# The front of a two-layer hybrid trunk step: order of loads, norm, conditioning blocks and first projections

## The chip, the cores and the metric

One core of a Trainium2 chip runs the kernel; the other cores are idle. The metric is the device time of one execution in microseconds, the median of several. The engines are named as the profile names them: PE is TensorE, DVE is VectorE, ACT is ScalarE, POOL is GpSimd, and SP is the engine that issues most of the loads and stores.

## What is computed

One inference step of a trunk of two layers, a Mamba-2 layer and a pooling layer, for 1024 prompt tokens and 8 sequences of 8 sample tokens, 1088 columns in all; the model is 1024 wide. Each layer begins in the same way, and only the beginning of the first layer is touched:

```python
sc  = silu(c)                                  # 9 conditioning rows: 8 samples, 1 prompt
mod = sc @ ada_w[i] + ada_b[i]
shift, scale, gate = split(mod, 3)
hn  = x * rsqrt(mean(x*x) + EPS) * norm_g[i] * (1 + scale) + shift
zxbcdt = hn @ w_in                             # z, x, B, C and the 32 step sizes dt
```

Behind it come the convolution, the scan over chunks, the gated norm, the output product and the pooling layer, all as before.

## The kernel before, in words

Activations lie with channels on partitions: `xs[k]`, k = 0..7, is a 128x1088 tile of x. Every product in full precision is split: an activation into `hh` (rounded to fp32r) and `hl` (the rest), a weight into a high and a low tile, and `mm1` (L187 to L192) issues three matmuls for one k and one chunk of columns. `CH` cuts the 1088 columns into 368, 368 and 352.

`setup` (L202) loads c, the eight x tiles, the vector constants `vec` and the other constants `kc` on SP, and issues 62 matmuls of ones (`warm`, L241) that keep TensorE active until data is there. `front` (L1394) then does the following.

- Sum of squares: ACT squares each x tile (L1403, L1407), DVE adds them into `rst` (L1408), the last in three chunks. For each chunk a matmul with ones adds over the partitions (L302, in `ms_log`), ACT takes the logarithm (L305) and the exponential (L318), which leaves 1/rms in `rst`.
- adaLN blocks: `ada_first(kt)` makes shift and scale of x tile kt. `ada_block` (L248) loads two halves of 512 KB (L257), makes eight small matmuls on 32-column strips of the array (L261, tile `am`; the profile shows two records for each), ACT copies the result to `mp` (L266), two tiny matmuls transpose it with constants of `kc` (L270), and DVE writes `shf` (L280) and `scl` (L281).
- `modulate(0, k, ...)` (L320): DVE multiplies x by scale and 1/rms (L325), ACT adds the shift and rounds (`hh`, L331), DVE makes the rest (`hl`, L332), ACT adds the shift to x itself (L333). The 64 sample columns have their own five small operations (L338 to L342).
- The loop over k: for each k the adaLN block of k + 2, `modulate` of k, 18 matmuls for the first two weight tiles of z (`pst`, named mm and p in the trace), and four strip matmuls of the step sizes (L1443, `pdt`), which read the unrounded x that L333 left. The first two weight tiles come whole (L121) and are split whole (L141, L145).
- Then come two more z tiles (`mm` with wh and wl), during which `act_sums_front` (L1471 to L1475) forms sums of x for the fast products that follow. POOL makes the sums of weights for those products (L1035 to L1042).

The order in which an engine executes is fixed before the launch: a scheduler takes, for each engine, the instruction that it expects to be ready, earlier ones in program order first. `tc.issue_after(ins)` adds that what is traced in its block stands behind `ins` on the same engine; it adds no wait for its end.

## Time and profile before

| | us |
|---|---|
| median of 3 runs (1590.49 to 1592.91) | 1590.76 |
| the profiled execution, its device time | 1591.15 |
| its span in the trace | 1589.0 |
| PE busy | 1568.2 |
| DVE busy | 1301.7 |
| ACT busy | 790.1 |
| POOL busy | 525.5 |

The span is what lies between the first and the last instruction of the trace; the 2.15 us beside it belong to launch and end. Times in the rows are counted from the start of the span. Matmuls overlap, so a busy time of PE is no proof of full use; the distance from one matmul's start to the next says more. In the rows of the timeline the columns are start, duration, engine, line, operation, tiles, shape, count, and in brackets the idle time before with what ended it. Rows of one kind that follow each other are merged, and then the duration is that of the whole run.

### The profile page before, as it was taken

How to read it: one execution, taken by the hardware profiler on the slowest of the kernel's cores; microseconds unless marked ns; L12 is line 12 of the kernel's file. 1: busy time of each engine (PE TensorE's matmuls, PEld its weight loads, DVE VectorE, ACT ScalarE, POOL GpSimd, SP SyncE). 2: the span in 40 equal slices, each digit the busy share in tenths (PEclk: the TensorE clock that was granted, in tenths of full speed). 3: DMA queues.
4: the chain of work that ended last, by engine and by line, in shares of the span. 5: the costliest groups of instructions: out<-in, count | busy, mean ns of one | idle time of the engine just before them, and what ended most of it. 6: DMA issues, size and time to landing. Idle time of an engine off the chain costs nothing.

```text
span 1589.0 us, 30720 instructions
## 1 busy us (share of the span) xinstructions
PE 1568.2 (99%) x11946; PEld 1505.1 (95%) x11946; DVE 1301.7 (82%) x2152; ACT 790.1 (50%) x1512; POOL 525.5 (33%) x558
## 2 busy tenths in 40 slices
PE   9999999999999999999999999999999999999997
PEld 7899999999999999989999999999999999999997
DVE  6874889887899989889888858988889777667886
ACT  6663344466766666665456348433333233233373
POOL 0133456522331413141211232366666530000241
PEclk9999999999999999999999999999999999999999
DMA  9422232365555565679999432232333379565783
GB/s 356 167 101 101 80 112 84 111 194 173 161 179 165 162 209 167 212 259 297 311 332 320 164 127 69 85 121 100 117 115 115 104 250 365 140 180 178 163 172 117
DMA packets 122304, 275.57 MB, mean 173 GB/s; under 512 B 18192, under 2 KB 59312, under 8 KB 122160
## 3 DMA queue, kind: packets, MB, share of 16 engines
q1 hardware_dynamic: 118128, 260.90, 48.4%
q0 software_dynamic: 4032, 12.72, 4.7%
q8 instruction: 94, 1.54, 0.4%
q14 instruction: 50, 0.41, 0.1%
HBM read 201.12 MB, written 70.23 MB: 171 GB/s over the span
## 4 chain that ended last, share of the span: by engine, by line
PE 85%; DVE 6%; issue 3%; DMA 3%; ACT 2%; POOL 1%; SPq 0%; DVEq 0%; ACTq 0%; POOLq 0%
PE st L1070 11%; PE st L1072 11%; PE st L1071 11%; PE mm L190 10%; PE mm L191 10%; PE mm L192 10%; PE op L1289 2%; PE op L1291 2%; PE op L1290 2%; PE y L641 2%; PE S L619 2%; PE y L645 1%; PE am L261 1%; PE tr L580 1%; PE tr L577 1%
## 5 line engine op out<-in xcount | busy, mean ns | idle before, releaser
L1072 PE MATMUL st<-hh,w 128*128 128x272 f32 x832 | 240.2, 289 | 0.0
L1070 PE MATMUL st<-hh,w 128*128 128x272 f32 x832 | 240.0, 288 | 0.0
L1071 PE MATMUL st<-hl,w 128*128 128x272 f32 x832 | 240.0, 288 | 0.0
L1070 PE MATMUL st<-t,w 128*128 128x272 f32 x624 | 179.6, 288 | 0.0
L1072 PE MATMUL st<-t,w 128*128 128x272 f32 x624 | 179.5, 288 | 0.0
L1071 PE MATMUL st<-t,w 128*128 128x272 f32 x624 | 179.2, 287 | 0.0
L190 PE MATMUL mm<-hh,wh 128*128 128x368 f32 (+1 forms) x528 | 178.9, 339 | 0.0
L191 PE MATMUL mm<-hl,wh 128*128 128x368 f32 (+1 forms) x528 | 174.0, 330 | 0.0
L192 PE MATMUL mm<-hh,wl 128*128 128x368 f32 (+1 forms) x528 | 173.2, 328 | 0.0
L1070 PEld LDWEIGHTS st<-hh,w 128*128 128x128 f32 x832 | 156.7, 188 | 0.0
L1071 PEld LDWEIGHTS st<-hl,w 128*128 128x128 f32 x832 | 156.7, 188 | 0.0
L1072 PEld LDWEIGHTS st<-hh,w 128*128 128x128 f32 x832 | 156.5, 188 | 0.0
L182 ACT ACTIVATE w<-wr 128x512 fp32r<-128x512 f32 x104 | 64.9, 629 | 165.5 <-PE st L1072 134.2
L627 POOL TENSOR_TENSOR hd<-h,cd 128x256 f32<-128x256 f32 x56 | 46.1, 824 | 285.9 <-DVE h L628 135.6
L1289 PE MATMUL op<-b,w 128*128 128x272 f32 x448 | 129.4, 289 | 0.0
L1290 PE MATMUL op<-b,w 128*128 128x272 f32 x448 | 128.8, 287 | 0.2 <-DVE b L1218 0.2
L1291 PE MATMUL op<-b,w 128*128 128x272 f32 x448 | 128.9, 288 | 0.0
L190 PE MATMUL mm<-gh,wh 128*128 128x368 f32 (+1 forms) x372 | 125.3, 338 | 0.0
L192 PE MATMUL mm<-gh,wl 128*128 128x368 f32 (+1 forms) x372 | 122.4, 329 | 0.0
L191 PE MATMUL mm<-gl,wh 128*128 128x368 f32 (+1 forms) x372 | 122.2, 328 | 0.1
L1070 PEld LDWEIGHTS st<-t,w 128*128 128x128 f32 x624 | 117.6, 189 | 0.1
L1072 PEld LDWEIGHTS st<-t,w 128*128 128x128 f32 x624 | 117.3, 188 | 0.0
(310 smaller groups left out, 4596.9 us busy)
## 6 DMA issues: line engine op xcount, KB each, us to landing
wr<-win SPq DMA_DIRECT2D x48, 512.0 KB, 3.8
wr<-pin SPq DMA_DIRECT2D x32, 512.0 KB, 3.8
acb<-acd SPq DMA_DIRECT2D x60, 256.0 KB, 4.4
wr<-pout SPq DMA_DIRECT2D x28, 512.0 KB, 5.2
x<-x1d SPq DMA_DIRECT2D x24, 544.0 KB, 6.7
x1d<-x SPq DMA_DIRECT2D x22, 544.0 KB, 6.2
wr<-pout POOLq DMA_DIRECT2D x20, 512.0 KB, 6.0
x<-xT SPq DMA_DIRECT2D x16, 544.0 KB, 6.7
```

Source lines behind the costliest of these rows:

```text
L182: self.last_hi = self.nc.scalar.activation(hi, src, AF.Copy)
L190: nc.tensor.matmul(ps[:, :n], hi[:, k, :], ah[:, a:a + n], start=first, stop=False)
L191: nc.tensor.matmul(ps[:, :n], hi[:, k, :], al[:, a:a + n], start=False, stop=False)
L192: nc.tensor.matmul(ps[:, :n], lo[:, k, :], ah[:, a:a + n], start=False, stop=last)
L619: nc.tensor.matmul(S[:, 256 * i:256 * i + 256], Bt, xde.rearrange("p r q -> p (r q)"), start=True, stop=True)
L627: nc.gpsimd.tensor_tensor(out=hd, in0=h[-1], in1=cd.unsqueeze(2).to_broadcast([P, 4, 64]), op=ALU.mult)
L1070: nc.tensor.matmul(ps[c][:, :QUART], hi[:, k], xh[:, t], start=(k == 0), stop=False)
L1071: nc.tensor.matmul(ps[c][:, :QUART], hi[:, k], xl[:, t], start=False, stop=False)
L1072: nc.tensor.matmul(ps[c][:, :QUART], lo[:, k], xh[:, t], start=False, stop=(k == 3))
L1289: nc.tensor.matmul(ps[:, :QUART], hi[:, k], xh, start=k == 0, stop=False)
L1290: nc.tensor.matmul(ps[:, :QUART], hi[:, k], xl, start=False, stop=False)
L1291: nc.tensor.matmul(ps[:, :QUART], lo[:, k], xh, start=False, stop=k == 7)
```

## The change

Loads: x tile 1 and c are issued by ACT, the rest by SP. Of `kc` only the 10 columns for the tiny transposing matmuls come first, then adaLN block 0, `vec`, and parts 0 and 1 (of 8) of the first two weight tiles; then adaLN block 1, the weights' other parts, block 2, `wdt` and the rest of `kc`. Blocks 3 to 7 are loaded from within the loop.

Norm: DVE adds squares 1 to 6 only; the eighth tile's squares are added on TensorE, as a second matmul into the same PSUM tile, chunk by chunk. The adaLN block 0 stands on TensorE behind the first two chunks, the third chunk's two matmuls stand around its transposing matmuls.

Weights: the first two tiles are split in parts 0-1, 2-3 and 4-7, each where it is near its use; the low half of 4-7 on POOL. The sample columns' product with 1/rms is made for all eight tiles on POOL.

Loop: k = 0 and k = 1 are modulated by chunks, and k = 0 runs chunk by chunk over both weight tiles. Block 1 stands behind the third group of matmuls of k = 0, block 2 behind the first group of k = 1. For k = 1 to 5 the step-size matmuls of k - 1 and then the adaLN block of k + 2 stand behind the matmuls of k; the step sizes of 5, 6 and 7 stand behind the matmuls of 7. ACT adds the shift to x one step later. `warm` has 52 matmuls instead of 62, and 4 instead of 8 later. The constants `cwh`, `adab1` and `an` are made later.

```diff
-        nc.sync.dma_start(ct, io["cT"])
         self.xs = []
         for k in range(8):
             t = self.slots.get("x")
-            nc.sync.dma_start(t, io["xT"][k])
+            if k == 1:
+                nc.scalar.dma_start(ct, io["cT"])
+            (nc.scalar if k == 1 else nc.sync).dma_start(t, io["xT"][k])
             self.xs.append(t)
+        self.adaq = []
+        self.kc = cp.tile([P, K_N], F32, tag="kc", name="kc")
+        self.kc_load(K_SEL9, K_SEL64)
+        self.ada_load(0)
         self.vec = cp.tile([P, V_N], F32, tag="vec", name="vec")
         nc.sync.dma_start(self.vec, io["vec"])
-        self.kc = cp.tile([P, K_N], F32, tag="kc", name="kc")
-        nc.sync.dma_start(self.kc, io["kc"])
...
+        self.wfirst = [self.wp.tile([P, 8, P], F32, tag="wr", bufs=3, name=self.name("wr")) for _ in range(2)]
+        self.first_load(0, 2)
...
-        self.warm(62)
+        self.warm(52)
...
+    def ada_load(self, m):
+
+        for hh in range(2):
+            self.adaq.append(self.slots.get("ada"))
+            self.nc.sync.dma_start(self.adaq[-1][:, :1024].rearrange("p (a b) -> p a b", a=4), self.io["adaA"][0, m][:, 4 * hh:4 * hh + 4, :])
+
+    def kc_load(self, a, e):
+
+        self.nc.sync.dma_start(self.kc[:, a:e], self.io["kc"][:, a:e])
+
+    def first_load(self, a, e):
+
+        for i, t in enumerate(self.wfirst):
+            self.nc.sync.dma_start(t[:, a:e], self.items[i][0][:, a:e])
+
+    def first_split(self, raw):
+
+        self.wslots += [self.slots.get("w0", F32R) for _ in range(2)]
+        hi, lo = (t[:, :1024].rearrange("p (k m) -> p k m", k=8) for t in self.wslots[-2:])
+
+        def part(a, e):
+            self.nc.scalar.activation(hi[:, a:e], raw[:, a:e], AF.Copy)
+            return lambda: (self.nc.gpsimd if a == 4 else self.nc.vector).tensor_tensor(out=lo[:, a:e], in0=raw[:, a:e], in1=hi[:, a:e].bitcast(F32), op=ALU.subtract)
+
+        return hi, lo, part
...
-                raws.append(self.slots.get("ada"))
-                nc.sync.dma_start(raws[hh][:, :1024].rearrange("p (a b) -> p a b", a=4), src[:, 4 * hh:4 * hh + 4, :])
+                raws.append(self.adaq.pop(0))
...
-            nc.scalar.activation(t[:, :pn], t[:, :pn], AF.Identity, bias=sh)
         if pn < n:
             s = slice(NP, TOK)
             ts = t[:, pn:n].rearrange("p (b i) -> p b i", i=8)
             eng = nc.gpsimd if l and k % 2 == 0 else nc.vector
-            eng.tensor_tensor(out=t[:, pn:n], in0=x[:, s], in1=rst[:, s], op=ALU.mult)
-            eng.tensor_tensor(out=ts, in0=ts, in1=self.scl[l][:, k, 0:8].unsqueeze(2).to_broadcast([P, 8, 8]), op=ALU.mult)
+            if l:
+                eng.tensor_tensor(out=t[:, pn:n], in0=x[:, s], in1=rst[:, s], op=ALU.mult)
+            with contextlib.nullcontext() if l else self.tc.issue_after(self.mod_x.ins):
+                eng.tensor_tensor(out=ts, in0=ts, in1=self.scl[l][:, k, 0:8].unsqueeze(2).to_broadcast([P, 8, 8]), op=ALU.mult)
             eng.tensor_tensor(out=ts, in0=ts, in1=self.shf[l][:, k, 0:8].unsqueeze(2).to_broadcast([P, 8, 8]), op=ALU.add)
...
         rst = sl.get("rst")
+        after = self.tc.issue_after
+        ms = [self.mm_tile() for _ in CH]
+
+        def add_up(c, sq, start):
+            a, n = CH[c]
+            return nc.tensor.matmul(ms[c][:, :n], self.ones, sq[:, a:a + n], start=start, stop=not start).ins
+
+        def root(c):
+            a, n = CH[c]
+            nc.scalar.activation(rst[:, a:a + n], ms[c][:, :n], AF.Ln, bias=self.eps, scale=1.0 / 1024)
+            return lambda: self.rstd(rst[:, a:a + n])
+
         with self.ln_set():
             nc.scalar.activation(rst, xs[0], AF.Square)
             for k in range(1, 8):
                 sq = self.raw_tile()
                 for a, n in CH if k == 7 else ((0, TOK),):
                     nc.scalar.activation(sq[:, a:a + n], xs[k][:, a:a + n], AF.Square)
-                    nc.vector.tensor_tensor(out=rst[:, a:a + n], in0=rst[:, a:a + n], in1=sq[:, a:a + n], op=ALU.add)
-            for a, n in CH:
-                self.ms_log(rst, rst, a, n, 1.0 / 1024, "mm", 3)
-                self.rstd(rst[:, a:a + n])
-        self.ada_first(0)
+                for a, n in CH if k == 6 else ((0, TOK),) if k < 6 else ():
+                    added = nc.vector.tensor_tensor(out=rst[:, a:a + n], in0=rst[:, a:a + n], in1=sq[:, a:a + n], op=ALU.add)
+            for c in range(2):
+                add_up(c, rst, True)
+                mm = add_up(c, sq, False)
+            self.adab1 = self.cp.tile([P, 48], F32, tag="adab1", name="adab1")
+            with after(added.ins):
+                nc.vector.tensor_scalar(self.adab1, self.vec[:, V_ADAB:V_ADAB + 48], 1.0, None, op0=ALU.add)
+            root(0)()
+            exp = root(1)
+            blk = self.ada_shift_scale(0, 0, False)
+            with after(mm):
+                next(blk)
+            with after(self.mp.ins):
+                exp()
+            with after(self.am):
+                add_up(2, rst, True)
+            for _ in blk:
+                pass
+            with after(self.sel):
+                mm = add_up(2, sq, False)
+            self.wslots = []
+            firsts = [self.first_split(t) for t in self.wfirst]
+            with after(self.mp.ins):
+                lower = [firsts[0][2](0, 2)]
+                exp = root(2)
+                exp()
+                lower.append(firsts[1][2](0, 2))
+        for t in xs:
+            nc.gpsimd.tensor_tensor(out=t[:, NP:TOK], in0=t[:, NP:TOK], in1=rst[:, NP:TOK], op=ALU.mult)
         self.hn = []
-
-        self.wslots = []
-        lower = [self.stream_split(i, True) for i in range(2)]
-        with self.tc.issue_after(self.sel):
-            self.warm(8, "mm", 3)
-        self.ada_first(1)
-        ws = [self.wsplit.pop(i) for i in range(2)]
+        with after(mm):
+            self.warm(4)
+        self.ada_load(1)
+        self.first_load(2, 8)
+        self.ada_load(2)
+        wdts = sl.get("wdt")
+        wdt = wdts[:, :256].rearrange("p (k m) -> p k m", k=8)
+        nc.sync.dma_start(wdt, io["wdt"])
+        self.kc_load(0, K_SEL9)
+        self.kc_load(K_SEL64, K_N)
+        ws = [f[:2] for f in firsts]
         self.wpos = 2
         pst = [[self.mm_tile() for _ in range(3)],
                [self.pp.tile([P, 512], F32, tag=t, bufs=b, name=self.name("p0")) for t, b in (("y", 2), ("y", 2), ("S", 1))]]
         pdt = self.pp.tile([P, 512], F32, tag="tr", bufs=2, name="pdt")
-        for k in range(8):
-            if k < 6:
-                self.ada_first(k + 2)
-            if k == 4:
-                self.stream_split(2)
-            if k == 6:
-                self.stream_split(3)
-            hi, lo = sl.get("hh", F32R), sl.get("hl", F32R)
-            for a, n in CH if k == 0 else ((0, TOK),):
-                last = self.modulate(0, k, xs[k], rst, hi, lo, a, n, xs[k][:, a:a + n])
-                if lower:
-                    lower.pop(0)()
-            self.hn.append((hi, lo))
-            for i in range(2):
-                for c in range(3):
-                    self.mm1(pst[i][c], ws[i], k, (hi, lo), CH[c], k == 0, k == 7)
+
+        def step_sizes(i):
             for j in range(4):
                 n = 320 if j == 3 else 256
-                nc.tensor.matmul(pdt[32 * j:32 * j + 32, :n], wdt[:, k, :], xs[k][:, 256 * j:256 * j + n],
-                                 start=k == 0, stop=k == 7, tile_position=(0, 32 * j))
+                ins = nc.tensor.matmul(pdt[32 * j:32 * j + 32, :n], wdt[:, i, :], xs[i][:, 256 * j:256 * j + n],
+                                       start=i == 0, stop=i == 7, tile_position=(0, 32 * j))
+            return ins
+
+        def unrounded(i):
+            return nc.scalar.activation(xs[i][:, :NP], xs[i][:, :NP], AF.Identity, bias=self.shf[0][:, i, 8:9])
+
+        cwh = self.gp.tile([P, 160], F32, tag="cwh", name="cwh")
+        self.cwh = cwh
+        for k in range(8):
+            if 0 < k < 6:
+                self.ada_load(k + 2)
+            if k in (4, 6):
+                with after(self.mod_hi.ins), after(last.ins):
+                    self.stream_split(k // 2)
+            hi, lo = sl.get("hh", F32R), sl.get("hl", F32R)
+            for a, n in CH if k < 2 else ((0, TOK),):
+                last = self.modulate(0, k, xs[k], rst, hi, lo, a, n, xs[k][:, a:a + n])
+                with after(self.mod_x.ins):
+                    for f in lower:
+                        f()
+                lower = []
+            if k > 1:
+                with after(self.mod_hi.ins):
+                    if k == 2:
+                        for f in firsts:
+                            f[2](4, 8)()
+                    unrounded(k - 1)
+            if k == 2:
+                with after(last.ins):
+                    nc.vector.tensor_scalar(cwh, self.vec[:, V_CW:V_CW + 160], 0.5, None, op0=ALU.mult)
+            self.hn.append((hi, lo))
+            for n, (c, i) in enumerate((c, i) for c in range(3) for i in range(2)) if k == 0 else enumerate((c, i) for i in range(2) for c in range(3)):
+                mm = self.mm1(pst[i][c], ws[i], k, (hi, lo), CH[c], k == 0, k == 7)
+                if k < 2 and n == (2, 0)[k]:
+                    with after(mm.ins):
+                        self.ada_first(k + 1)
+                    if k:
+                        with after(self.mp.ins):
+                            lower = [f[2](2, 4) for f in firsts]
+                            unrounded(0)
+            if 0 < k < 6:
+                with after(mm.ins):
+                    mm = step_sizes(k - 1)
+                with after(mm.ins):
+                    self.ada_first(k + 2)
+        unrounded(7)
+        with after(mm.ins):
+            for k in range(5, 8):
+                step_sizes(k)
```

## Rows read from the trace of the kernel before

**Rows 1.** The page: busy time of TensorE, its share of the span, instructions.

```profile
PE 1568.2 (99%) x11946; PEld 1505.1 (95%) x11946; DVE 1301.7 (82%) x2152; ACT 790.1 (50%) x1512; POOL 525.5 (33%) x558
```

**Rows 2.** Busy time by stretch: length, then five engines, clock, DMA share, GB/s.

```profile
2.00:3.00 1.00, 1.00 (x7) 1.00 (x6) 0.20 (x1) 0.06 (x2) 0.00 (x0) 1.00 0.86 181
...
5.00:6.00 1.00, 1.00 (x8) 1.00 (x7) 0.00 (x0) 0.71 (x1) 0.00 (x0) 1.00 1.02 409
...
68.00:72.00 4.00, 4.00 (x26) 4.00 (x25) 4.00 (x7) 1.77 (x6) 0.00 (x0) 1.00 0.42 166
```

**Rows 3.** Timeline of PE, from the warm matmuls to the first product.

```profile
1.06 16.34 PE L245 MATMUL warm<-ones 128*128 128x128 f32 x124 [1.06 <-DVE ones L217]
...
17.24 1.99 PE L302 MATMUL ms<-rst,ones 128*128 128x368 f32 x6
...
20.32 0.64 PE L261 MATMUL am<-ada,scp 128*32 128x256 f32 x8 [0.52 <-DMA ada<-adaA]
...
21.47 0.61 PE L270 MATMUL am<-kc,mp 128*128 128x9 f32 x4 [0.50 <-ACT mp L266]
...
23.94 0.95 PE L190 MATMUL mm<-hh,w 128*128 128x368 f32 x2
```

**Rows 4.** Timeline of ACT and DVE in the same stretch.

```profile
15.23 1.30 ACT L1407 ACTIVATE raw<-x 128x368 f32<-128x368 f32 x3 [0.28 <-DMA x<-xT]
...
16.55 1.43 DVE L1408 TENSOR_TENSOR rst<-rst,raw 128x368 f32<-128x368 f32 x3
...
21.03 0.38 ACT L266 ACTIVATE mp<-am 128x256 f32<-128x256 f32 x1 [0.18 <-PE am L261]
...
22.65 1.12 DVE L325 SCALAR_TENSOR_TENSOR x<-x,scl,rst 128x368 f32<-128x368 f32 x2
```

**Rows 5.** Timeline of PE in the loop and behind it.

```profile
43.34 0.74 PE L1443 MATMUL pdt<-x,wdt 128*32 128x256 f32 x8
...
48.47 0.75 PE L1443 MATMUL pdt<-x,wdt 128*32 128x256 f32 x8
...
48.93 1.15 PE L261 MATMUL am<-ada,scp 128*32 128x256 f32 x16
...
50.01 0.44 PE L190 MATMUL mm<-hh,w 128*128 128x368 f32 x1
...
62.62 0.74 PE L1443 MATMUL pdt<-x,wdt 128*32 128x256 f32 x8
...
66.46 0.74 PE L1443 MATMUL pdt<-x,wdt 128*32 128x256 f32 x8
...
67.13 0.44 PE L190 MATMUL mm<-hh,wh 128*128 128x368 f32 x1
...
67.41 0.33 PE L191 MATMUL mm<-hl,wh 128*128 128x368 f32 x1
...
71.76 0.33 PE L190 MATMUL mm<-hh,wh 128*128 128x368 f32 x1
```

**Rows 6.** Timeline of ACT and DVE, from adaLN block 6 to the next step.

```profile
50.18 0.39 ACT L266 ACTIVATE mp<-am 128x256 f32<-128x256 f32 x1 [0.84 <-PE am L261]
...
51.59 0.23 DVE L280 TENSOR_SCALAR shf<-am,vec 128x9 f32<-128x9 f32 x1 [0.71 <-PE am L270]
...
52.05 1.28 DVE L325 SCALAR_TENSOR_TENSOR x<-x,scl,rst 128x1024 f32<-128x1024 f32 x1
...
53.37 1.15 ACT L331 ACTIVATE hh<-x,shf 128x1024 fp32r<-128x1024 f32 x1 [0.35 <-DVE x L325]
...
54.78 1.28 DVE L332 SCALAR_TENSOR_TENSOR hl<-x,shf,hh 128x1024 fp32r<-128x1024 f32 x1
```

**Rows 7.** Timeline of POOL and DVE late in the loop, and DVE behind it.

```profile
57.28 1.33 POOL L1036 TENSOR_TENSOR sw<-sw,wr 128x512 f32<-128x512 f32 x1
...
57.37 2.32 DVE L325 SCALAR_TENSOR_TENSOR x<-x,scl,rst 128x1024 f32<-128x1024 f32 x1
...
62.45 1.35 DVE L1471 TENSOR_TENSOR x<-x 128x544 f32<-128x544 f32 x2
```

More of the change, by code (lines that the diff above doesn't have):

```diff
@@ L191, in mm1 @@
         nc.tensor.matmul(ps[:, :n], hi[:, k, :], al[:, a:a + n], start=False, stop=False)
-        nc.tensor.matmul(ps[:, :n], lo[:, k, :], ah[:, a:a + n], start=False, stop=last)
+        return nc.tensor.matmul(ps[:, :n], lo[:, k, :], ah[:, a:a + n], start=False, stop=last)
     def mm3(self, ps, w, acts, ch):
@@ L260, in ada_block @@
             for j in range(4):
-                nc.tensor.matmul(pm[32 * j:32 * j + 32, :256], self.scp[:, j + 4 * hh, :], raws[hh][:, 256 * j:256 * j + 256],
-                                 start=(hh == 0), stop=(hh == 1), tile_position=(0, 32 * j))
+                am = nc.tensor.matmul(pm[32 * j:32 * j + 32, :256], self.scp[:, j + 4 * hh, :], raws[hh][:, 256 * j:256 * j + 256],
+                                      start=(hh == 0), stop=(hh == 1), tile_position=(0, 32 * j))
+        self.am = am.ins
         if src is not None:
@@ L265, in ada_block @@
         mp = self.cp.tile([P, 256], F32, tag="mp", bufs=1, name=self.name("mp"))
-        nc.scalar.activation(mp, pm[:, :256], AF.Copy)
+        self.mp = nc.scalar.activation(mp, pm[:, :256], AF.Copy)
         yield
@@ L472, in dt_phase @@
         an = self.gp.tile([P, 1], F32, tag="an", name="an")
-        nc.scalar.activation(an, self.vec[:, V_ALOG:V_ALOG + 1], AF.Exp)
-        nc.vector.tensor_scalar(an, an, -1.0, None, op0=ALU.mult)
+        with self.tc.issue_after(self.mod_hi.ins), self.tc.issue_after(self.mod_x.ins):
+            nc.scalar.activation(an, self.vec[:, V_ALOG:V_ALOG + 1], AF.Exp)
+            nc.vector.tensor_scalar(an, an, -1.0, None, op0=ALU.mult)
         nc.vector.tensor_scalar(dd, uu, 2.0, None, op0=ALU.add)
```

11 lines of the change are left out of this document (2 added, 9 removed).

## The prediction

> **What bounds the kernel now.** I read the page first: TensorE is busy 1568.2 of 1589.0 us [rows 1], so only time in which TensorE does not do wanted work can be won. Busy time alone would hide that here, because the 62 matmuls of ones count as busy. So the timeline of TensorE comes next: ones until 17.4 us, the norm's three sums at 17.24, the second half of adaLN block 0 at 20.32 after a wait for its load, and the first wanted product only at 23.94 [rows 3]. From there to 67.13, where the next weights begin [rows 5], runs the loop that is changed. Behind it TensorE is full (4.00 of 4.00 us) [rows 2], so what the loop ends earlier, the kernel ends earlier, unless the next stage gives it back.
>
> Inside the loop three distances matter [rows 5]. From 67.41 to 71.76 lie 26 matmuls of 368 columns: 0.167 us each, and by columns 0.160 for 352; one k has 12 and 6 of them, 2.97 us. Step 7, without an adaLN block, takes 66.46 - 62.62 = 3.84, so the step sizes cost 0.87, of which 48.93 - 48.47 = 0.46 is their own and 0.41 is lost in changing tile shape and back. Step 3, with a block, takes 48.47 - 43.34 = 5.13: a block costs 1.29, of which 0.87 for the strips (50.01 - 48.47, against 67.13 - 66.46 without them) and 0.42 for the transposing ones. The loop's own work is thus 8 x 3.84 + 7 x 1.29 = 39.75 us of the 43.19 that it takes. The other 3.44 are waits and block halves standing apart in steps 0 to 2.
>
> **The change: the first product.** The last tile of x is squared from 15.23 on, as it lands, and block 0 is there only at 20.32 [rows 3, 4]. Between the two came block 0 (1.05 MB) and 0.67 MB of constants and step-size weights. At 409 GB/s [rows 2] the block alone needs 2.6 us, so with nearly all constants behind it it lands near 17.8. Two load queues I count at nothing: by 5 us the engines are at a DMA share of 1.02; at 2 to 3 us they show 0.86 with 181 GB/s, which leaves at most about half a microsecond, and the next step would hide it.
>
> That next step is the norm. The three chunk adds of the last tile began at 16.55 and take 1.43, 0.48 each [rows 4]. With tile 6 as the last one on DVE, in chunks, its first chunk is done near 15.5 (16.55, less 0.1 for two constants that move away, less the two chunks of 0.48 behind it). The 52 warm matmuls end between 14.8 (52/62 of 16.34) and 15.7 (if the ten omitted ran at the loop's 0.17). I take 15.7 for the start of the sums. Three chunk sums took 1.99, 0.66 each [rows 3]. Four of them now stand ahead of block 0, the price of adding the last squares here: 15.7 + 2.65 = 18.35, behind the load. From a block's first matmul to its copy on ACT takes 50.18 - 48.93 = 1.25 [rows 5, 6], from the copy to the transposing matmuls 0.44 [rows 3, 4]: 20.04. One more chunk sum of 0.66 stands in between and begins 1.08 after the block, so 20.1. From there to DVE's first modulation took 1.18, and from that to the first product 1.29 [rows 3, 4]: 22.57. The third chunk's logarithm and exponential fall on ACT just there. By the 0.38 for 256 columns [rows 4] one of them in front costs 0.5, none costs 0; I take half. First product at 22.8 (22.6 to 23.1), **1.1 us earlier**.
>
> **The loop's own work.** 8 x 2.97 for the products; six groups of step sizes instead of eight (five beside blocks, one of three at the end), 6 x 0.87 + 2 x 0.46; seven blocks, 7 x 1.29; and blocks 1 and 2 stand alone, two shape changes of 0.41 more. That is 39.75, as before: what the grouping at the end saves, the lone blocks take.
>
> **The waits.** These were 3.44, and here lies the rest of the gain.
>
> Step 1: modulation and rest of step 0 are 1.28 each on DVE when whole [rows 6], about 0.4 more in chunks. Two weight quarters (0.7), the sample columns (0.5) and the next scale and shift (0.46) follow, and POOL's eight products take DVE's turn for 0 to 3 us, say 1.0. From 21.3 that is 26.9, plus 1.2 for the first chunk's modulation and rounding: 28.1. TensorE is through step 0 and block 1 at 22.8 + 2.97 + 1.29 + 0.41 = 27.5. Wait 0.6 (0 to 2). The loads keep up: at 409 GB/s block 1 lands near 21.4 (wanted at 24.6), the weights' other parts near 23.3, block 2 near 25.9 (wanted at 29). For the unrounded x, made a step later on ACT, I count nothing: the step sizes that read it stand behind 18 matmuls; without that cover it would cost its 1.15.
>
> Steps 2 to 6: block k + 2 now stands behind the matmuls of k, one step later than before. The chain after it is in [rows 5, 6]: products go on at 50.01, copy 50.18, shift 51.59, modulation 52.05, rounding 53.37 to 54.52. So the next k can begin 4.5 us after the block. A step with a block and step sizes covers this with 5.13. For what disturbs it I put 0.6 in all (0 to 4): see the rival below.
>
> Step 7: block 7 stands between steps 5 and 6, and step 6 has only 2.97 + 0.42 + 0.1 = 3.5 us of matmuls, since its step sizes are held back until after step 7. The chain of 4.5 is not covered: **a new wait of 1.0**, 0.6 if the transposing matmuls go in at once, 1.4 if the rest (`hl`, another 1.3) is asked for early.
>
> Sum of waits 2.2 instead of 3.44. The loop ends at 22.8 + 39.75 + 2.2 = 64.75 instead of 67.13: 2.4 us. The profiled execution took 1591.15 (span 1589.0 and 2.15 beside it) and would take 1588.75; the median lies 0.39 below it, so the forecast is 1590.76 - 2.4 = **1588.4**. The constants made later on DVE and ACT (0.1 to 0.3 each) come where both have idle time, and are counted at nothing; on the chain at step 7 they would cost those 0.3.
>
> **A rule against the change.** POOL and DVE do get in each other's way: beside POOL's weight sum at 57.28, DVE's modulation took 2.32 instead of 1.28 [rows 6, 7]. Before, this hit step 7's modulation with TensorE far behind, so it cost nothing; now the same chain has 0.6 us of slack, or none. The Trainium skill, "SBUF — State Buffer", section "SBUF: two separate sides", says why: DVE operations with two SBUF inputs and POOL's share one pair of ports under an exclusive lock held for the whole instruction, so that the loser blocks fully rather than slowing down. The row agrees, with 1.04 us lost beside one POOL operation of 1.33. By the rule every product given to POOL could be taken back from DVE in full, and then waits like the slower rival's follow.
>
> **The rivals.**
>
> 1. The waits close. The transposing matmuls go right behind the copy (chain 4.1), POOL falls into DVE's idle time, no exponential stands in front. First product 22.57, waits 0.3 + 0 + 0.6: the loop ends at 63.2, 3.9 us earlier, **1586.9**. For it: in step 3's row shift came 1.4 us after the copy though the copy itself is 0.39 long, so there is room. Against: step 7's missing cover is arithmetic.
>
> 2. Slower. The late blocks and the lock meet: each chain grows by 1.04, to 5.5, and `hl` behind it again, so that steps 2 to 5 wait 1.2 each, step 7 2.0 and step 1 1.7. Waits 8.5, the loop ends at 71.0, **1594.7**. It decides from waits of 4.6 in all (3.44 + 1.1) for a loss, and of 7.8 for a loss one can measure. For it: 57.37 in [rows 7]; POOL's weight sums start as soon as the weight buffers come free, which is earlier now, in steps 4 and 5. Against: POOL has few operations there, and one step's slack of 0.6 takes half of each.
>
> 3. Given back. DVE's sums of x began at 62.45, 4.7 us ahead of the loop's end [rows 5, 7]. Now step 7 begins at 60.0 (64.75 less 2.97 and 1.79), its rest ends near 61.5, and the lead is 3.2. If the next stage needs all of the old lead, 1.5 is lost there: **1589.9**. Against: TensorE has 24 us of ordinary products before the sums are due.
>
> 4. It doesn't do what it says: the scheduler, which knows only expected times, leaves block 0's chain where it was (first product at 23.9, the rest as forecast): **1589.5**.
>
> **How the numbers follow.** Forecast 0.42, rival 1 0.34, rival 2 0.11, rival 3 0.07, rival 4 0.06. About 0.2% (3.2 us) is what a measurement of this kernel can tell from no change, so faster means below 1587.6 and slower above 1593.9. Faster: 0.29 of rival 1 and 0.05 of the forecast's lower end, 0.34. Slower: 0.08, the harder part of rival 2. Same: 0.58. The forecast's own range is 1587.4 to 1590 from its bounds; for 8 in 10 it reaches down through most of rival 1 (1585.5, with the loads earlier as well) and up to rival 2's mild end, 1592.
>
> **What would show it.** First product at 22.8 (right if 22.4 to 23.2); block 0 no longer waiting for its load but for the chunk sums; first product of step 1 about 5.3 us after that; steps 2 to 5 at 5.1 each; TensorE idle for about 1 us ahead of step 7, released by ACT's `hh`; three groups of step sizes at the end, 0.46 apart; next weights at 64.7. I am wrong if TensorE is idle between steps 2 and 6, if step 7 doesn't wait, or if the gain at the loop's end is not there at the end of the span.

## The result and the profile after

The changed kernel takes **1596.69 us** (median; 1594.08 to 1599.08) beside 1591.23 of the kernel before on the same chip: a ratio of 1.0032 [1.0022, 1.0041], so slower by 5.5 us, where 1588.4 was forecast. The profiled execution took 1594.88 with a span of 1592.8.

TensorE's timeline of the changed kernel at the front, to be read against [rows 3] (columns as there):

```profile
1.06 14.53 PE L271 MATMUL warm<-ones 128*128 128x128 f32 x104 [1.06 <-DVE ones L220]
16.45 0.89 PE L1432 MATMUL mm<-rst,ones 128*128 128x368 f32 x2 [0.86 <-DVE rst L1446]
...
19.12 1.07 PE L286 MATMUL am<-ada,scp 128*32 128x256 f32 x16
...
20.82 0.51 PE L296 MATMUL am<-kc,mp 128*128 128x9 f32 x4
...
23.19 0.43 PE L190 MATMUL mm<-hh,w 128*128 128x368 f32 x1 [0.27 <-ACT hh L357]
```

Block 0 no longer waits for its load, and the first product starts at 23.19 instead of 23.94, 0.75 us earlier. The loop behind it loses this and more. The same timeline at those places of the loop where TensorE waits, and the start of the next weights, against [rows 5]:

```profile
24.37 0.43 PE L191 MATMUL mm<-hl,w 128*128 128x368 f32 x1 [0.59 <-DVE hl L358]
...
25.98 1.07 PE L286 MATMUL am<-ada,scp 128*32 128x256 f32 x16
...
30.02 0.43 PE L190 MATMUL mm<-hh,w 128*128 128x368 f32 x1 [0.96 <-ACT hh L357]
...
61.01 0.43 PE L191 MATMUL mm<-hl,w 128*128 128x368 f32 x1 [0.77 <-DVE hl L358]
...
65.84 0.76 PE L190 MATMUL mm<-hh,w 128*128 128x368 f32 x3 [0.81 <-ACT hh L357]
...
71.09 0.43 PE L190 MATMUL mm<-hh,wh 128*128 128x368 f32 x1
```

The next weights start at 71.09 instead of 67.13, 3.96 us later, and the span is 3.8 longer. Behind the loop nothing is lost and nothing given back in these two traces: from the next weights to the span's end lie 1521.9 us before (1589.0 - 67.13) and 1521.7 after. (In the traces of the other kernels below this stretch takes 1519.8 to 1523.2.) So for the profiled execution the answer lies in the eight steps. Their lengths, each from one step's first product to the next one's, and for step 7 to the next weights; "forecast" is the own work of the prediction's sum plus its waits, laid out by step:

| step | 0 | 1 | 2 | 3 | 4 | 5 | 6 | 7 | sum |
|---|---|---|---|---|---|---|---|---|---|
| before | 8.84 | 6.94 | 5.16 | 5.13 | 5.16 | 4.28 | 3.84 | 3.84 | 43.19 |
| forecast, own work | 4.67 | 6.83 | 5.13 | 5.13 | 5.13 | 5.13 | 2.97 | 4.76 | 39.75 |
| forecast with waits | 5.27 | 6.83 | 5.28 | 5.28 | 5.28 | 5.28 | 3.97 | 4.76 | 41.95 |
| after | 6.83 | 6.73 | 6.18 | 5.64 | 5.17 | 5.57 | 6.53 | 5.25 | 47.90 |

Above the own work lie 47.90 - 39.75 = **8.15 us of waits**, where the forecast put 2.2: 2.2 in step 0, 1.05 in step 2, about 0.5 each in steps 3, 5 and 7, and 3.6 in step 6; step 1 gives back 0.1. The kernel before has its 3.44 in steps 0 to 2 and nothing behind them. The changed one still has 3.1 there and 5.0 more in steps 3 to 7. DVE and POOL in step 6:

```profile
57.33 1.22 DVE L145 TENSOR_TENSOR wl<-wr,wh 128x1024 fp32r<-128x1024 f32 x1
58.46 1.30 DVE L366 TENSOR_TENSOR x<-x,scl 128x64 f32<-128x64 f32 x1
59.69 1.27 DVE L358 SCALAR_TENSOR_TENSOR hl<-x,shf,hh 128x1024 fp32r<-128x1024 f32 x1
60.88 1.29 DVE L367 TENSOR_TENSOR x<-x,shf 128x64 f32<-128x64 f32 x1
62.10 0.21 DVE L306 TENSOR_SCALAR shf<-am,vec 128x9 f32<-128x9 f32 x1
...
62.55 0.85 DVE L369 TENSOR_TENSOR hl<-x,hh 128x64 fp32r<-128x64 f32 x1
63.33 1.27 DVE L351 SCALAR_TENSOR_TENSOR x<-x,scl,rst 128x1024 f32<-128x1024 f32 x1
```

```profile
57.62 2.06 POOL L1063 TENSOR_TENSOR sw<-wr 128x512 f32<-128x512 f32 x1 [17.22 <-DMA wr<-win]
59.76 2.33 POOL L1064 TENSOR_TENSOR sw<-sw,wr 128x512 f32<-128x512 f32 x1
62.05 1.26 POOL L1068 TENSOR_TENSOR wr<-wr,wr 128x512 f32<-128x512 f32 x1
```

Operations of 64 columns that take 0.21 to 0.23 elsewhere take 1.30, 1.29 and 0.85 here, and modulation 7 begins only at 63.33; its rounding releases TensorE at 65.84. POOL and DVE take turns: each line of POOL ends about where a stretched line of DVE does, while the two long lines of DVE between them (1.22 and 1.27) keep their length. The Trainium skill, "SBUF — State Buffer", section "SBUF: two separate sides", has this as an exclusive lock held for a whole instruction; the trace agrees, with 0.22 against 1.30 for the same operation.

Step 2 shows the same once more, DVE and then POOL:

```profile
38.55 0.28 DVE L307 TENSOR_SCALAR scl<-am,adab,vec 128x9 f32<-128x9 f32 x1
...
39.17 1.34 DVE L1525 TENSOR_SCALAR cwh<-vec 128x160 f32<-128x160 f32 x1
40.42 1.27 DVE L351 SCALAR_TENSOR_TENSOR x<-x,scl,rst 128x1024 f32<-128x1024 f32 x1
```

```profile
37.44 2.96 POOL L263 TENSOR_TENSOR w<-wr,w 128x512 fp32r<-128x512 f32 x2 [10.54 <-ACT w L262]
```

Scale 3 is there at 38.83, but the constants `cwh`, which take 0.24 with POOL away, hold DVE until modulation 3 begins at 40.42. By these lines the lock can account for step 2's 1.05 as well; no kernel below tests this by itself.

### The profile page after: what moved, and what is told of

It is laid out like the page before. It is cut to its first block, busy times and chain, and to the rows that moved or that the text cites. A ratio compares the mean times of both kernels' runs of the same rounds, so it can differ in the third digit from the quotient of the medians.

```text
span 1592.8 us, 30706 instructions
## 1 busy us (share of the span) xinstructions
PE 1568.8 (98%) x11924; PEld 1504.2 (94%) x11924; DVE 1305.2 (82%) x2149; ACT 790.4 (50%) x1516; POOL 531.2 (33%) x568
## 4 chain that ended last, share of the span: by engine, by line
PE 85%; DVE 6%; issue 3%; ACT 2%; DMA 2%; POOL 1%; SPq 0%; DVEq 0%; ACTq 0%; POOLq 0%
PE st L1098 11%; PE st L1100 11%; PE st L1099 11%; PE mm L190 11%; PE mm L191 10%; PE mm L192 10%; PE op L1317 2%; PE op L1319 2%; PE op L1318 2%; PE y L669 2%; PE S L647 2%; PE y L673 1%; PE tr L608 1%; PE am L286 1%; PE tr L605 1%
```

## The experiments

The theory was that two things together make the loop longer: adaLN blocks that come a step later (late blocks), and POOL's sums of weights beside DVE (the lock). The rivals were that one of them alone does it, that the front does it (loads, ones, clock), or that it is not in the loop. The first four kernels ran with the kernel before on one chip, as did the next four, the next three and the last one.

**The change again.** The changed kernel with no edit.

> The changed kernel as it is, for a second trace and more times. If what the first trace shows is the rule, the steps again start near 23.2, 30.0, 36.8, 42.9, 48.6, 53.7, 59.3, 65.8 us and the next weights near 71.1, 4.0 us later than before. The times went from 1594.1 to 1599.1 with a mean granted clock between 0.998 and 0.995; if the spread belongs to the clock, a trace with the lower one shows a stretch at the lower level, and if it belongs to the waits, the steps start at other times.

Median 1595.93, ratio 1.0028 [1.0017, 1.0040]. The loop took 47.91 with each step as in the first trace, but it began at 25.71 instead of 23.19. The timeline of TensorE, and its clock by stretch (columns as [rows 2]), of this run:

```profile
1.06 13.32 PE L271 MATMUL warm<-ones 128*128 128x128 f32 x104 [1.06 <-DVE ones L220]
17.29 1.16 PE L1432 MATMUL mm<-rst,ones 128*128 128x368 f32 x2 [2.91 <-DVE rst L1446]
18.24 1.43 PE L1432 MATMUL mm<-raw,ones 128*128 128x368 f32 x2
```

```profile
18.00:21.00 3.00, 3.00 (x6) 1.66 (x5) 0.30 (x2) 1.08 (x2) 0.00 (x0) 0.50 1.02 392
```

The ones end at 14.38, TensorE is idle for 2.91 us, and the sums then run at a granted clock of 0.50, the 1.2 GHz level: 1.2 us from one to the next instead of 0.62. First product 2.5 us later: the sums start 0.84 later, and from the first sum to the first product lie 8.42 instead of 6.74. In the first trace of after the ones ended at 15.59, the gap was 0.86 and the clock stayed at 1.00. Three kernels below have the same front (POOL waits, blocks early, and the changed kernel with blocks half a step earlier); with gaps of 2.03 to 2.17 their traces show a clock of 0.83 from 15 to 25 us, as this one does.

**POOL waits.** POOL's first sum of weights waits for DVE's last rest of step 7.

```diff
-            nc.gpsimd.tensor_tensor(out=s[:, f], in0=z[:, f], in1=z[:, l], op=ALU.add)
+            ins = nc.gpsimd.tensor_tensor(out=s[:, f], in0=z[:, f], in1=z[:, l], op=ALU.add)
+            if self.mod7 is not None:
+                self.tc.add_manual_dep(ins.ins, self.mod7.ins.name, ...)
...
+        self.mod7 = last
```

> Only change: POOL's first sum of weights waits until DVE has made the last rest of step 7. Theory (late adaLN blocks meet POOL on the ports that DVE needs): the two small sample operations on DVE in step 6 take 0.22 instead of 1.3 us, modulation 7 begins about 2.5 us earlier, step 7 starts near 63.4 and the next weights near 68.6, 2.5 us before the changed kernel. Rival (late blocks alone, their chain is too long with or without POOL): next weights stay at 70.5 to 71.1. Rival (POOL alone is the cause): next weights at 67 or before.

Median 1594.54, ratio 1.0021 [1.0011, 1.0031]. Step 6 took 4.58 instead of 6.53, and no other step moved by over 0.02. DVE and POOL of this kernel:

```profile
60.13 0.22 DVE L366 TENSOR_TENSOR x<-x,scl 128x64 f32<-128x64 f32 x1
...
61.49 0.22 DVE L367 TENSOR_TENSOR x<-x,shf 128x64 f32<-128x64 f32 x1
...
63.04 1.28 DVE L351 SCALAR_TENSOR_TENSOR x<-x,scl,rst 128x1024 f32<-128x1024 f32 x1
```

```profile
67.04 1.71 POOL L1063 TENSOR_TENSOR sw<-wr 128x512 f32<-128x512 f32 x1 [24.98 <-DVE hl L369]
```

So the lock costs **1.95 us** in step 6. The loop is still 45.94. By its time alone this kernel can't be told from the change, since their intervals overlap.

**Blocks early, in the changed kernel.** Blocks 3 and 4 behind step 1, then block k + 3 behind step k; their loads are issued earlier to match.

```diff
...
-                    self.ada_first(k + 2)
+                    for m in (3, 4) if k == 1 else (k + 3,) if k < 5 else ():
+                        self.ada_first(m)
```

> Only change: adaLN blocks 4 to 7 stand one step earlier (3 and 4 behind step 1, then block k+3 behind the matmuls of k, k = 2 to 4), so that each modulation has a whole step more of cover. Theory: step 1 is longer by a block (1.3 us), then steps 2 to 4 take their own work, 5.1 each, steps 5, 6, 7 take 3.8, 3.1 and 3.0, and the next weights start near 65.5, 5.5 us before the changed kernel and 1.6 before the kernel before. Rival (POOL on the ports is the cause): the waits of 2 us around POOL's sums stay and the next weights start at 68 or later.

Median 1593.38, ratio 1.0009 [0.9998, 1.0019]: 2.6 us better than the change, with intervals that just overlap. Steps 5 to 7 fell from 17.35 to 12.28, of which 1.29 is a block that has left them, but steps 2 and 3 rose from 11.82 to 14.15, where that block now lies. Loop 45.14. POOL's first sum begins only at 63.17 here, behind modulation 7 (61.64), and that modulation keeps its 1.28.

**Blocks late, in the kernel before.** The converse: the kernel before with block k + 2 behind the step sizes of k and nothing else.

```diff
-            if k < 6:
-                self.ada_first(k + 2)
...
+            if k < 6:
+                with self.tc.issue_after(ins.ins):
+                    self.ada_first(k + 2)
```

> The kernel before with one part of the change: each adaLN block of k+2 stands behind the step sizes of k instead of ahead of the matmuls of k. Nothing moves to POOL, loads and norm are the old ones. Theory: steps 0 to 2 hardly change, but modulations 5 to 7 lose their cover, POOL's sums (57 us) now hit the chain of step 7, and the next weights start 2 to 4 us later than 67.1, the kernel is slower by as much. Rival (the new front, its chunks and POOL's new products are the cause): next weights at 67.1 to 67.6, time as before.

Median 1593.47, ratio 1.0015 [1.0005, 1.0025]. The loop took 45.70 instead of 43.19: steps 5 to 7 took 5.55, 4.56 and 5.44 instead of 4.28, 3.84 and 3.84, of which 1.29 is block 7, which now lies there. POOL, DVE, and TensorE's wait in step 7, of this kernel:

```profile
61.75 2.15 POOL L1036 TENSOR_TENSOR sw<-sw,wr 128x512 f32<-128x512 f32 x1
```

```profile
62.67 1.31 DVE L339 TENSOR_TENSOR x<-x,scl 128x64 f32<-128x64 f32 x1
64.02 1.19 DVE L340 TENSOR_TENSOR x<-x,shf 128x64 f32<-128x64 f32 x1
```

```profile
65.55 0.43 PE L190 MATMUL mm<-hh,w 128*128 128x352 f32 x1 [0.96 <-ACT hh L341]
```

The late blocks without the rest of the change thus cost about half of what it loses in the loop (2.5 of 4.7), and they bring the lock with them: POOL's sums, which cost the kernel before nothing, now stretch DVE's operations for the sample columns of step 7, and TensorE waits 0.96 for these. How much of the 2.5 would stay with POOL held back was not tried.

**More ones.** The changed kernel with 62 warm matmuls instead of 52.

```diff
-        self.warm(52)
+        self.warm(62)
```

> The changed kernel with 62 warm matmuls instead of 52, nothing else. Theory (the gap of up to 2.9 us between the 52 matmuls and the first chunk sum is what lowers TensorE's clock in some executions): the gap shrinks to about 1.2 us or closes, the granted clock stays at 1.00 from 15 to 25 us, the first product stands between 23.2 and 24.1, never at 25, and the times spread less, median near 1594.8, with the loop's steps as before (47.9 in all). Rival (the spread comes from elsewhere, as the low stretches near 700 and 1000 us): times spread from 1592.7 to 1599 as with 52.

Median 1595.51, ratio 1.0024 [1.0014, 1.0034]. The clock stayed at 1.00 in the front, but the ones now end at 17.95 and stand in front of the sums; the first product came at 24.42. In step 6 TensorE waited 1.40 us for the sample columns:

```profile
64.71 0.48 PE L190 MATMUL mm<-hh,w 128*128 128x352 f32 x1 [1.40 <-ACT hh L368]
```

Behind this wait the granted clock was 0.66 from 65 to 70 us, and the loop took 48.72. Filling the gap with ones is no repair.

**One load queue.** The changed kernel with c and all of x issued by SP, c first, as before.

```diff
+        nc.sync.dma_start(ct, io["cT"])
...
-            if k == 1:
-                nc.scalar.dma_start(ct, io["cT"])
-            (nc.scalar if k == 1 else nc.sync).dma_start(t, io["xT"][k])
+            nc.sync.dma_start(t, io["xT"][k])
```

> The changed kernel with c and all x tiles loaded from SP, c first, as before the change. Theory (c, caught between x tiles, lands at 4.8 instead of 2.7 us, and ACT's table load and first square wait for it): first square at 5.3 instead of 6.6, first chunk sum near 15.7 instead of 16.45 or 17.3, the gap behind the warm matmuls under 1.5 us, clock 1.00, first product near 22.4, loop unchanged 47.9, median near 1593.5. Rival (the second queue brings the last x tile 1.1 us earlier, 14.1 instead of 15.2, and that counts): first chunk sum later than 16.4, first product at 23.2 or later.

Median 1594.96, ratio 1.0022 [1.0012, 1.0031]. ACT of the changed kernel, then ACT and TensorE of this one:

```profile
5.00 0.26 ACT L226 ACTIVATE cth<-ct 128x72 f32<-128x72 f32 x1 [2.04 <-DVE ct L225]
5.28 1.28 ACT L336 ACT_TABLE_LOAD   x1
6.58 1.11 ACT L1440 ACTIVATE rst<-x 128x1088 f32<-128x1088 f32 x1
...
14.14 1.30 ACT L1444 ACTIVATE raw<-x 128x368 f32<-128x368 f32 x3 [0.26 <-DMA x<-xT]
```

```profile
5.32 1.11 ACT L1439 ACTIVATE rst<-x 128x1088 f32<-128x1088 f32 x1 [1.07 <-DMA x<-xT]
...
15.18 1.30 ACT L1443 ACTIVATE raw<-x 128x368 f32<-128x368 f32 x3 [0.23 <-DMA x<-xT]
```

```profile
15.69 0.89 PE L1431 MATMUL mm<-rst,ones 128*128 128x368 f32 x2 [0.24 <-DVE rst L1445]
...
22.53 0.44 PE L190 MATMUL mm<-hh,w 128*128 128x368 f32 x1 [0.28 <-ACT hh L356]
```

Two queues bring the last tile of x 1.04 us earlier (14.14 against 15.18), but c later: the silu of c is at 5.00 instead of 2.69, ACT's table load for the squares stands behind it, and the first square starts at 6.58 instead of 5.32. DVE's chain of adds then ends later, though the last tile is early. With one queue the chunk sums start at 15.69 and the first product at 22.53. The loop lost nothing more and won nothing (47.96), and by its time alone this kernel can't be told from the change either. The Trainium skill, "DMA: Bandwidth & Descriptors", section "Issuing engines are not separate DMA queues", says that issuing from several engines saves only the time to issue. Part of the 1.04 may be that, as SP is through with issuing x at 5.09 instead of 5.80. But c, issued at 0.74 or 0.75 in both kernels, was 2.3 us later on the second queue, and that the page doesn't have; the measurement decides.

**Loads in the kernel before.** The kernel before with block 0 loaded ahead of the other constants and of `wdt`.

```diff
+        nc.sync.dma_start(self.kc[:, K_SEL9:K_SEL64], io["kc"][:, K_SEL9:K_SEL64])
+        self.ada0 = [self.slots.get("ada") for _ in range(2)]
+        for hh in range(2):
+            nc.sync.dma_start(self.ada0[hh]..., io["adaA"][0, 0]...)
...
```

> The kernel before with one part of the change: block 0 is loaded behind the 10 columns of constants that it needs, ahead of the other constants, the step-size weights and the rest. Theory (the first product was held by block 0's load): block 0 is there by 18, the first product stands at 22.3 to 22.8 instead of 23.94, the loop takes its 43.2, the next weights start near 65.8, 1.3 us before, median near 1590.1. Rival (the three logarithms and exponentials on ACT and the warm matmuls hold it): first product at 23.5 or later, time as before. Part of the loop could be lost if blocks 1 and 2 now come later: they are 0.5 MB further back, 1.2 us.

Median 1592.61, ratio 1.0013 [1.0004, 1.0022]. Block 0's matmuls start at 19.45 in one run of 16 records, without a wait for the load, yet the first product stays at 23.94: the transposing matmuls wait for the copy on ACT until 21.46, behind the exponentials there. The weights come later for it, and step 0 grows from 8.84 to 10.07. The load of block 0, which I took for the limit, was one of two that end together: in the kernel before, the block's matmuls end at 20.96 and the exponentials at 20.85.

**Both repairs.** One load queue and POOL's wait in the changed kernel.

> The changed kernel with two repairs: c and x from SP alone, and POOL's first weight sum behind modulation 7. If the two effects add: first product near 22.4, loop 47.9 less 1.95 = 45.95, next weights near 68.4, 2.7 us earlier than the changed kernel's first trace and 1.2 later than before; median near 1592. Rival (they overlap): 70 or later.

Median **1591.67**, ratio 1.0003 [0.9993, 1.0012]: level with the kernel before. First product 23.19, loop 45.87, next weights at 69.06. Two edits that touch neither the order of the blocks nor the norm take back the loss: this interval lies wholly below both of the changed kernel's. The first product is no earlier than in the first trace of after, because the last tile of x came late in this execution (its squares start at 16.52, 15.18 with one queue alone); the clock stayed at 1.00.

**The constants early.** That kernel with `cwh` made early, not beside POOL's low halves of the weights in step 2, where it took 1.34 us (L1525 at 39.17 in the trace of after).

```diff
+                nc.vector.tensor_scalar(self.cwh, self.vec[:, V_CW:V_CW + 160], 0.5, None, op0=ALU.mult)
...
-            if k == 2:
-                with after(last.ins):
-                    nc.vector.tensor_scalar(cwh, ...)
```

> e8_repairs with one edit more: the halved conv weights (DVE's product of 160 columns, L1525 at 39.17 in the trace after, 1.34 us there and 0.24 elsewhere) are made early, behind the halves of block 1, and no longer in step 2 beside POOL's low halves of the weights (L263, 2.96 us each). If POOL's work stretches DVE's there and modulation 3 waits for it, step 2 of the loop falls from 6.91 by about 1.1 to 5.7 to 5.9 us, steps 3 to 7 stay within 0.3 us, the next weights start at 67.9 to 68.2 (69.06 in e8_repairs) and the median lies 0.6 to 1.1 us under e8_repairs's 1591.7: 1590.6 to 1591.1, level with the kernel before. The rival: modulation 3 waits for its own block 3 and step sizes, which come late whatever POOL does; then step 2 stays at 6.7 to 6.9 and the time at 1591.7.

A miss. Step 2 stayed at 6.90, and the median was 1593.34, ratio 1.0007 [0.9998, 1.0016]. DVE and TensorE of this kernel:

```profile
37.23 1.31 DVE L368 TENSOR_TENSOR hl<-x,hh 128x64 fp32r<-128x64 f32 x1
39.98 0.23 DVE L305 TENSOR_SCALAR shf<-am,vec 128x9 f32<-128x9 f32 x1 [1.43 <-PE am L295]
```

```profile
39.36 0.51 PE L295 MATMUL am<-kc,mp 128*128 128x9 f32 x4
```

DVE was idle for 1.43 us: shift 3 waited for TensorE's transposing matmuls, not for the constants. The loop ends 0.58 earlier than in the repaired kernel (68.48), by a front that is as much earlier. The median is 1.7 higher, but the intervals of the two kernels overlap, so no difference between them is shown.

This miss doesn't settle step 2 of the changed kernel. There block 3 stands whole ahead of step 2's products (35.61); in the repaired kernel its second half stands behind the first of them (37.32), `cwh` ends at 40.39 and the transposing matmuls end at 40.46. With two chains that end together, taking one away shows nothing of what it costs where it is the longer one.

**Blocks half a step earlier.** The kernel of the constants with the step sizes of k - 1 and block k + 2 behind the third group of step k; and the changed kernel with that edit alone.

```diff
-            if 0 < k < 6:
-                with after(mm.ins):
-                    mm = step_sizes(k - 1)
-                with after(mm.ins):
-                    self.ada_first(k + 2)
+                if 0 < k < 6 and n == (5 if k == 1 else 2):
+                    with after(mm.ins):
+                        ss = step_sizes(k - 1)
+                    with after(ss.ins):
+                        self.ada_first(k + 2)
```

> e9_cwh with the late adaLN work moved forward inside its step: the step sizes of k-1 and adaLN block k+2 stand behind the third of the matmul groups of step k (k of 2 to 5; in step 1 behind the last, as after), so about half a step (2.4 us) earlier than after. If what step 5, 6 and 7 wait for is the chain that starts at the late block (block, DVE's shift and scale, modulation, halves), the waits of steps 3 to 7 close: step 7's start no longer stands behind a wait of over 0.3 us, the loop of steps 3 to 7 falls from 25.0 us in e8_repairs (43.54 to 69.06, less 0.5) to 23 to 24, the next weights start at 65.0 to 66.5, and the median is 1588 to 1589.8, 0.1 to 0.2 per cent faster than before. The rival: TensorE itself pays for the block in the middle of a step (the block's matmuls wait there for step k+1's silu or product and hold the step up) as much as the cover brings; then single steps of 5.7 us and more stay, the next weights start at 67.5 to 69 and the median is within 0.7 us of e9_cwh.

> The kernel after with nothing changed but the place of the step sizes of k-1 and of adaLN block k+2: behind the third group of step k's matmuls (k of 2 to 5) instead of behind the sixth. POOL still starts its weight sums in step 6 and two queues still bring c and x. If the missing cover of the late blocks is a cause of its own, the step lengths 4, 5 and 7 (5.17, 5.57, 5.25 after) fall to 4.3 to 5.2 and the loop from 47.90 to 45 to 46.5; the wait in step 6 (6.53) falls too if modulation 7 is then made before POOL's sums start at 57.6, and stays at over 6 if POOL's start moves forward with it. The median is then 1594 to 1595.5. If only the lock of POOL and DVE counts, the loop stays at 47 and over and the median at 1596.

The first missed: median 1595.07, ratio 1.0018 [1.0009, 1.0027]. Steps 6 and 7 took 2.96 and 4.96, all covered, but steps 2 and 3 took 8.36 and 7.02, with a wait of 1.42 for a rest of DVE; block 4 and half of block 3 fall into step 2. The second held for the loop: 46.26 instead of 47.90, with step 6 at 4.77; median 1594.07, ratio 1.0012 [1.0003, 1.0021]. The lock is still there: modulation 7 takes 2.33 instead of 1.28 beside POOL, and TensorE waits for it:

```profile
65.92 0.76 PE L190 MATMUL mm<-hh,w 128*128 128x368 f32 x3 [1.64 <-ACT hh L357]
```

Step 6 thus took 6.53 in the changed kernel, 4.58 with POOL held back, 4.77 with the blocks half a step earlier, and 2.96 with both (and the other edits of that kernel). Each edit takes about as much with the other as without it, 1.95 or 1.81 for POOL and 1.76 or 1.62 for the blocks, of which 0.42 are block 7's transposing matmuls, which move to step 5. So half a step of cover does not take the lock's price; the whole step of the blocks-early kernel kept modulation 7 clear of POOL.

**No POOL in step 2, block 1 earlier.** The repaired kernel with the low halves of parts 4 to 7 on DVE, and block 1 behind the first group of step 0 instead of the third.

```diff
-            return lambda: (self.nc.gpsimd if a == 4 else self.nc.vector).tensor_tensor(
+            return lambda: self.nc.vector.tensor_tensor(
...
-                if k < 2 and n == (2, 0)[k]:
+                if k < 2 and n == (0, 0)[k]:
```

> e8_repairs with two edits. One: the low halves of the weights' parts 4 to 7 are made by DVE instead of POOL (two operations of 512 columns), so that POOL does nothing in step 2. Two: adaLN block 1 stands behind the first instead of the third group of step 0's matmuls. In e9_cwh step 2 kept its 6.90 us though the constants no longer lay beside POOL; there DVE's rest of the sample columns (L368, 64 columns) still took 1.31 us beside POOL's L262 (36.74, 2.97 for two) instead of 0.23, TensorE's third chunk waited for it at 38.60, and the transposing matmuls of block 3 stood behind that chunk. If that reading is right, L368 falls to 0.23, modulation 3 starts 1.0 to 1.4 us earlier after the start of step 2, and step 2 takes 5.4 to 5.9 us; if step 2 is held by the place of block 3 alone, it stays at 6.7 to 6.9. Block 1 earlier: its copy, shift and modulation 1 move forward by up to 1.6 us until DVE's rests of step 0 (to 26.9 in e8_repairs) are in front; step 0 takes 5.4 to 6.2 instead of 6.72. Both together: loop of 43.6 to 44.4 instead of 45.9, next weights at 66.3 to 67.3, median 1589.8 to 1591, at or a little under the kernel before; with the second reading 1591.2 to 1592.

Median **1591.43**, ratio 0.9996 [0.9987, 1.0005]: the best of the variants, and no different from before. TensorE and DVE:

```profile
27.76 0.43 PE L190 MATMUL mm<-hh,w 128*128 128x368 f32 x1
...
35.48 0.76 PE L190 MATMUL mm<-hh,w 128*128 128x368 f32 x3 [0.88 <-ACT hh L356]
```

```profile
36.67 0.22 DVE L368 TENSOR_TENSOR hl<-x,hh 128x64 fp32r<-128x64 f32 x1
```

Step 0 took 5.56 instead of 6.72 (22.20 to 27.76), with no wait at its end: there block 1's place was the cause, as the other edit acts in step 2. But step 1 took 7.72 instead of 6.72; the wait went on to the next chain, block 2's. In step 2 the rest of the sample columns was back at 0.22, as expected, and the step still took 6.62: ACT's copy of block 3 stood behind the weights' high halves and the unrounded x, and TensorE's transposing matmuls behind the products. ACT's copy ends at 37.93, DVE's own work at 38.25 and the transposing matmuls at 39.01. Three things end there within about a microsecond, and taking one away brought 0.3 of the 1.0 to 1.4 that I expected.

## Why the prediction was wrong

**First product: right by its steps, but the load queues were mis-sized.** The forecast was 22.8 (22.6 to 23.1). The kernel with one queue and no other edit shows 22.53, its chunk sums 15.69 against 15.7; the other four with one queue show 22.20 to 23.19, the last of these with the late tile of x. "Two load queues I count at nothing" was wrong: I looked at bandwidth, not at who waits for c. With 52 ones and two queues the sums start at 16.45 to 17.29 in five traces, with one queue at 15.54 to 15.88 in five. In the first trace of after the first product came 0.66 later for it (23.19 against 22.53), in the run whose clock fell 3.2.

**The ones and the clock: seen and not priced.** I worked out that the 52 ones end between 14.8 and 15.7 and that the sums start at 15.7, but gave a gap no price. It was 0.86 in one trace and 2.03 to 2.91 in four others, and there TensorE fell to 1.2 GHz for about 3 us, which made the way from the sums to the first product 1.6 to 1.7 us longer (8.36 to 8.42 against 6.74). That is a cost that comes in some executions only; four of the five traces with 52 ones and two queues show it, and none of the five with one queue does.

**The loop's own work: right where nothing waits.** Step 1 took 6.73 against 6.83, step 4 5.17 against 5.13, and steps 3 and 4 with both repairs 5.14 and 5.16. Nothing was lost downstream, so rival 3 falls, and rival 4 with it, since block 0's chain did move.

**The waits: the step that failed.** The forecast put 2.2 where 8.15 lay.

- Step 0 (0.6 forecast, 2.2 measured). I counted DVE's queue to 26.9. DVE was through at 27.04 and then idle for 1.24, waiting for block 1's transposing matmuls: that block stands behind the third group, which waited for two rests. Its chain, 25.98 to 30.02, was not in my sum; the last kernel shows that its place decides, though there the wait reappears in step 1. DVE's line, of after:

```profile
28.27 0.23 DVE L306 TENSOR_SCALAR shf<-am,vec 128x9 f32<-128x9 f32 x1 [1.24 <-PE am L296]
```

- Step 7's new wait, 1.0 forecast ahead of it: 0.81 there, and 0.79 with POOL held back, where step 6 took 4.58 against 2.97 + 1.0, and 0.42 for transposing matmuls that fall into it. That "arithmetic" was right.
- Steps 2 to 6, "0.6 in all (0 to 4)": the mis-sized term. It came to 4.6, with the 1.0 forecast ahead of step 7 taken off. Without the lock's 1.95, which the kernel with POOL held back shows, step 6 would have kept to the forecast within 0.6; step 2's 1.05 has the lock in its chain too, by its lines only. The row for the lock stood in [rows 7] and I used it in rival 2, but as one hit of 1.04 on one modulation. In fact POOL's three sums follow each other without a gap (57.62 to 63.31), and each of the three 64-column operations of DVE in that time waits until one of them is over: together 2.8 us more than alone. My reason against it, "one step's slack of 0.6 takes half of each", looked at one hit per step.

**Rival 2 was the case that came**, with a sum of waits of 8.5 against 8.15 and a loop end of 71.0 against 71.09; its point of decision, 4.6 for a loss, holds too. That the sum fits so well is in part luck, since its places were not right: steps 3 and 4 lost little, as POOL was idle there for 17 us, and POOL's sums of weights began later than before (57.62 against 55.56), not earlier. The lock struck in step 6 and, by its lines, in step 2, and block 1's chain in step 0. I gave it 0.11. Its time of 1594.7 is that of the profiled execution (1594.88); the median lies 1.8 above that. A front that fell to 1.2 GHz in some of the timed executions would do that, and so might the two stretches at 0.79 that the second trace shows behind the loop (696 to 704 and 1000 to 1008 us), but the timelines of the others are not there to show it.

**What stays open.** The two repairs leave 45.87 in the loop against 43.19 before, and the gain in front (0.75 to 1.74 us earlier) doesn't pay for it. By the step lengths the late blocks are the larger part of that: with POOL held back, steps 5 to 7 still take 2.36 more than their own work (15.22 against 12.86), where the kernel before waits for nothing, and steps 0 to 2 wait 3.7, about as long as before. What lies in these three steps is shown for step 0 only. How step 2 would run with all three of its late ends moved at once was not tried; nor was the new front with the blocks as early as before.

## What to carry to other kernels

Moving a producer one step later removes slack from every chain behind it; then price not the one chain but each engine that can lengthen it, and above all an engine whose long operations lie beside it with no gap, since each short operation in that time may wait for a whole long one. An operation that is hidden today (POOL's sums at step 7 here) has to be priced again when what it hides behind moves. And when a load changes its queue, look for the small load that heads a chain (c, then the table load, then the squares) before counting bytes.

## What the runs showed of the hardware

- Pauses of 2.03, 2.15, 2.17 and 2.91 us on TensorE, each after 13 us of ones, were followed by a granted clock of 0.50 from 18 to 21 us; pauses of 0.85 to 1.09 in the same place were not. A pause of 1.40 later on (64.71, the kernel with more ones) was followed by such a fall too.
- Not only DVE's two-input operations stretch beside POOL. The halved constants (`cwh`, one input, 160 columns in fp32) took 1.34 us beside POOL and 0.24 with POOL away. The Trainium skill, "SBUF — State Buffer", section "SBUF: two separate sides", counts a DVE operation in a two-port mode among those that take the lock, beside those with two inputs; these rows agree with that if this one runs in such a mode, which no row names.
- The same eight tiles of x from two queues instead of one were in 1.04 us earlier, while the silu of c, from the second queue, began 2.3 us later than with c at the head of the only one (5.00 against 2.69).
